# TensorE's order in a step of an attention: value products of blocks 3 to 1 last, transposes of block 0 among the second head's scores

## The chip, the cores and the metric

The kernel runs on one NeuronCore of a Trainium2 chip. The metric is the device time of one execution in microseconds (us), shown as the median of several runs; smaller is better. Five engines work beside each other, each through a queue of its own in order: TensorE (PE in the profile, its weight loads shown apart as PEld), VectorE (DVE), ScalarE (ACT), GpSimd (POOL) and SyncE (SP), which here only issues DMAs.

## The reference

The program is a trunk of two layers over 512 tokens of width 1024 in float32. Layer 0 mixes tokens with a convolution module, layer 1 with an attention in three branches; a gated feed-forward network (FFN) follows each. The change lies in the attention. Cut to what matters:

```
s_s = einsum('bgrqd,bgqkd->bgrqk', qc, k_s) * scale     # selected blocks
p_s = masked_softmax(s_s, tok <= t[:, None])
o_s = einsum('bgrqk,bgqkd->bgrqd', p_s, v_s)
...
s_w = einsum('bgrqd,bgkd->bgrqk', qc, kw) * scale       # window of 512
p_w = masked_softmax(s_w, mask_w)
o_w = einsum('bgrqk,bgkd->bgrqd', p_w, vw)
...
return g[0] * o_c + g[1] * o_s + g[2] * o_w
```

There are 16 query heads of width 64 in 4 groups that share keys and values. At 512 tokens there are 8 blocks to select from and up to 16 may be selected, and the window is as long as the sequence: so the branches "selected" (br = 1) and "window" (br = 2) are both plain causal attentions over all tokens, each with keys and values of its own. The third branch, over 31 compressed blocks (`o_c`), is small.

## The kernel before, in words

The function `nsa` does the attention. After the projections it runs a loop over 16 units, `us`: a unit is one pair of heads `j` (8 pairs) in one branch `br` (1, 2). The two heads of a pair are called first and second here (`par` = 0, 1; `ua`, `ub`). Each head has four rows of 128 queries, t = 0 to 3, and four blocks of 128 keys, kc = 0 to 3; being causal, row t needs keys up to 128(t + 1).

The loop is a software pipeline. Step n makes the scores and the softmax of unit n, the transposes of unit n - 1, the value products of blocks 3, 2 and 1 of unit n - 1 and those of block 0 of unit n - 2. Scores for steps 1 to 15 (unit 0 has its scores ahead of the loop), transposes for steps 1 to 16, and step 17 has only the last value products.

- `score` (L1694) makes one row of scores: two matmuls per row (L1704, L1705; the query operand `St` holds a high and a low part) into a PSUM bank `S`, of which there are three in turn. VectorE adds the mask and finds the row's extreme while it copies the scores to SBUF (L1707, tile `Pm`), ScalarE takes the exponential in place with its sum (L1708). After rows 2 and 0, `weigh` (L1712) takes the reciprocal of two rows' sums on VectorE (L1718), and GpSimd multiplies both rows by it and by the gate (L1722).
- `flip` (L1725) transposes four 128 x 128 pieces of weighed probabilities by TensorE into a PSUM tile `T` (L1735) and copies it to SBUF, tile `t`, by VectorE (L1738) or ScalarE (L1740). `t2` has block 2 of both heads, `t1` blocks 1 and 3 of one head, `t0` block 0 of one head. The PSUM tiles come from a pool of three, `p2`, which the fill work uses too.
- `values` (L1744) multiplies the transposed probabilities with the values into the output `O` (L1761): half as many output partitions per head, the two heads side by side. In units of branch 1 the three products of the compressed branch (L1753 to L1755, operands `pch`, `pcl`) go ahead.
- `run_fill` (L1777) takes the next of five pieces of work for a later pair of heads (`q_pair`, L1473): query moves by DMA on SP's queue (L1485), casts of the operand `St` (L1496, L1498, L1499), scores, softmax and transposes of the compressed branch. A pair's pieces are spread over two and a half steps, two calls a step.

TensorE's order is as written: each of these matmuls is kept in program order (`pe`). What the other engines do, and in which order, is put in order by the compiler's planner from the dependences. So a change of TensorE's order in the text is a change of its queue, and the other queues can change with it.

Behind the loop follow the output projection (`proj_tile`, matmuls `pp`) and the FFN of layer 1.

Of the kernel before, what the change touches and what calls it, by code (L numbers as in the profile page):

```python
# [120 lines left out]
def trunk(ctx: ExitStack, tc: tile.TileContext, A, out):  # L121
    nc = tc.nc
# [8 lines left out]
    def nm(s):  # L131
        cnt[0] += 1
        return f"{s}_{cnt[0]}"
# [78 lines left out]
    def w_hi(i):  # L212
        if i in split or i >= len(units):
            return
        w_dma(i)
        cols = units[i][1]
        hi = wp.tile([P, 1024], F32R, tag="wh", name=f"wh{i}", bufs=2)
        lo = wp.tile([P, 1024], F32R, tag="wl", name=f"wl{i}", bufs=2)
        parted(after(nc.scalar.activation(hi[:, :cols], raws[i][:, :cols], AF.Copy), pin.get(AF)))  # L219
        split[i] = (hi, lo)  # L220

    def w_lo(i=None):
        i = state["next"] if i is None else i
        if i in los or i not in split:
            return
        cols = units[i][1]
        hi, lo = split[i]
        parted(after(nc.vector.tensor_tensor(lo[:, :cols], raws[i][:, :cols], hi[:, :cols], ALU.subtract), pin.get(ALU)))  # L228
        los.add(i)
# [969 lines left out]
    def nsa(acc, gnext):  # L1199
# [481 lines left out]
        def offs(t):  # L1681
            return P * t * (t + 1) // 2
# [11 lines left out]
        def score(U, t):  # L1694
            j, par, br = U["j"], U["par"], U["br"]
            g = 2 * (j // 4) + par
            stk, ks_, kl = qst[j, par], kst[br, g], klo[br, g]
            w = P * (t + 1)
            n = max(w, 256)
            tq = slice(t * P, (t + 1) * P)  # L1700
            mx, sm = U["mx"][:, t:t + 1], U["sm"][:, t:t + 1]
            n_s[0] += 1
            ps = pS[len(pS) > 1 and n_s[0] % 3 == 0].tile([P, T], F32, tag="S", name=nm("S"))
            pe(nc.tensor.matmul(ps[:, :n], stk[:, tq], ks_[:, :n], start=True, stop=False))  # L1704
            pe(nc.tensor.matmul(ps[:, :n], stk[:, tq], kl[:, :n], start=False, stop=True))  # L1705
            Pt = U["P"][:, offs(t):offs(t) + w]
            at_[ALU] = nc.vector.tensor_tensor_reduce(Pt, ps[:, :w], mask[:, T - w:], 1.0, 3e38, ALU.add, ALU.min, mx)  # L1707
            at_[AF] = nc.scalar.activation(Pt, Pt, AF.Exp, bias=mx, scale=-1.0, accum_out=sm)  # L1708
            if t % 2 == 0:
                weigh(U, t)  # L1710
# [14 lines left out]
        def flip(parts, tag, eng):  # L1725

            pt = p2.tile([P, T], F32, tag="p2", name=nm("T"))
            t_ = box["q4"].tile([P, T], F32, tag=tag, name=nm("t"), bufs=2 if tag != "t2" else 1)
            c = 0
            for u, kc in parts:  # L1730
                n = T - P * kc
                u[kc] = t_[:, c:c + n]
                for t in range(kc, 4):
                    o = offs(t) + P * kc
                    pe(nc.tensor.transpose(pt[:, c:c + P], u["P"][:, o:o + P], ident))  # L1735
                    c += P
            if eng is nc.vector:
                eng.tensor_copy(t_, pt)  # L1738
            else:
                eng.activation(t_, pt, AF.Copy)  # L1740
# [3 lines left out]
        def values(Us, kcs):  # L1744


            j, br = Us[0]["j"], Us[0]["br"]
            a = j // 4
            if br == 1 and kcs[0] == 3:
                ob[j] = (p2, pO)[j % 2].tile([P, T], F32, tag="O", name=nm("O"), bufs=1)  # L1750
                ph, pl = pcT[j // 2]
                ch, cl = vcb[a, j % 2]
                pe(nc.tensor.matmul(ob[j], ch, ph, start=True, stop=False))  # L1753
                pe(nc.tensor.matmul(ob[j], ch, pl, start=False, stop=False))
                pe(nc.tensor.matmul(ob[j], cl, ph, start=False, stop=False))  # L1755
            o = ob[j]
            for kc in kcs:
                last = br == 2 and kc == 0
                for par in range(2):
                    g = slice((2 * a + par) * DH, (2 * a + par + 1) * DH)  # L1760
                    pe(nc.tensor.matmul(o[par * 64:par * 64 + 64, P * kc:], vf[br][:, kc, g], Us[par][kc], start=False,  # L1761
                                        stop=last))
                if last:
                    h_ = op.tile([P, T], F32R, tag=f"o{j}", name=nm("oh"))
                    l_ = oha.tile([P, T], F32R, name=nm("ol"))
                    nc.scalar.activation(h_, o, AF.Copy)
                    nc.vector.tensor_tensor(l_, o, h_, ALU.subtract)
                    oh.append(h_)
                    ol.append(l_)
# [7 lines left out]
        def run_fill():  # L1777
            if fill_:
                fill_.pop(0)()

        def start(n):
            nonlocal fill_
            j, br = us[n]
            U[n] = [begin(j, par, br) for par in range(2)]
            if n % 4 == 0 and n // 4 + 1 < 4:
                fill_ = q_pair(n // 4 + 1)
# [13 lines left out]
        for n in range(1, N + 2):  # L1800
            S = n < N
            F = n <= N
            if S:
                start(n)

            def sc_(par, *ts):
                if S:
                    for t in ts:
                        score(U[n][par], t)

            sc_(0, 3, 2)
            if F:
                ua, ub = U[n - 1]
                flip(((ua, 2), (ub, 2)), "t2", nc.scalar)
            if n > 1:
                values(U.pop(n - 2), (0,))
            sc_(0, 1, 0)
            if F:
                flip(((ua, 1), (ua, 3)), "t1", nc.vector)
            sc_(1, 3)  # L1820
            if F:
                flip(((ub, 1), (ub, 3)), "t1", nc.vector)
            sc_(1, 2)
            if n == 1:
                qp0[4]()
            run_fill()
            if F:
                values(U[n - 1], (3, 2, 1))
            sc_(1, 1, 0)
            if F:  # L1830
                flip(((ua, 0),), "t0", nc.scalar)
                flip(((ub, 0),), "t0", nc.scalar)
            run_fill()
            if n in W_AT:
                pin.update(at_)
                if n == W_AT[0]:
                    w_hi(state["next"])
                    w_lo()
# [19 lines left out]
    cx0.close()  # L1858
    acc = ffn(acc, V_NM1, 0)
    acc = nsa(acc, V_NF1)  # L1860
    ffn(acc, None, 1)
    hx[0].close()
# [157 lines left out]
```

## Time and profile before

| | us |
|---|---|
| median of 3 runs | 1239.86 |
| lowest, highest run | 1237.12, 1243.43 |
| the profiled execution, its time | 1243.02 |
| its span in the profile | 1241.2 |
| TensorE busy in the span (8519 matmuls) | 1206.9 (97%) |
| VectorE, ScalarE, GpSimd busy | 903.1, 603.8, 245.3 |
| value products of step 1 / step 15 start at | 703.13 / 835.90 |
| the output projection starts at | 847.72 |

How to read it: a line of the timeline or of the chain is start, duration, engine, line of the kernel, operation, output tile <- input tiles, shape, count; square brackets give the engine's idle time just ahead and the instruction that ended it. A line of the waits is engine, line and what it waited for: us in total, times, longest. A line of groups is line, engine, operation, tiles, shapes, count, busy us, mean ns, idle us ahead and who ended it. Matmuls are pipelined, so their recorded durations overlap; the time that one takes from the next is the difference of two starts.

### The profile page before, as it was taken

What the parts mean: (1) busy time and instruction counts of PE and PEld (TensorE: products, weight loads), DVE (VectorE), ACT (ScalarE), POOL (GpSimd) and SP (SyncE); (2) the same over time, 40 slices, a digit from 0 to 9 for tenths busy, and PEclk for the clock granted to TensorE, in tenths of its full rate; (3) what the DMA queues carried; (4) which work ended last, traced back from release to release, by engine and by line L of the source; (5) the groups of instructions that cost most, each with busy time, mean ns of one, the idle gap of its engine ahead of it and who ended that gap; (6) DMA issues with size and microseconds to landing.
All of it is one profiled execution on the core that took longest, in us unless ns stands there. A gap on an engine that the chain in (4) does not pass through costs nothing.

```text
span 1241.2 us, 22077 instructions
## 1 busy us (share of the span) xinstructions
PE 1206.9 (97%) x8519; PEld 1047.2 (84%) x8519; DVE 903.1 (73%) x1722; ACT 603.8 (49%) x1116; POOL 245.3 (20%) x349
## 2 busy tenths in 40 slices
PE   9999899999999999999998999999999999999998
PEld 6787778799999999887677876667878999998998
DVE  6995598877777576856686787763587777776775
ACT  5221464455555444543443577773354555554443
POOL 2011002011111103102332466552000111110120
PEclk9999999999999999999999899999999999999999
DMA  8748628277777668454266101005323877774882
GB/s 314 264 131 285 172 88 235 92 180 186 181 179 178 162 204 147 97 182 113 60 143 165 26 18 44 1 18 143 112 85 108 198 179 182 190 177 119 225 166 90
DMA packets 88378, 181.11 MB, mean 146 GB/s; under 512 B 36816, under 2 KB 38480, under 8 KB 86736
## 3 DMA queue, kind: packets, MB, share of 16 engines
q1 hardware_dynamic: 66816, 109.99, 29.1%
q0 software_dynamic: 21456, 69.71, 24.8%
q8 instruction: 67, 1.10, 0.4%
q14 instruction: 39, 0.32, 0.1%
HBM read 165.60 MB, written 5.80 MB: 138 GB/s over the span
## 4 chain that ended last, share of the span: by engine, by line
PE 77%; DVE 10%; DMA 3%; issue 3%; ACT 3%; SPq 2%; POOL 1%; DVEq 0%; ACTq 0%; POOLq 0%
PE st L915 27%; PE st L1105 10%; PE pp L281 7%; PE pp L279 7%; PE pp L280 6%; PE O L1761 3%; PE st L281 2%; PE st L280 2%; PE st L279 2%; PE cpe L540 2%; DVE wl L228 1%; DVE Pm L1707 1%; PE T L1735 1%; PE S L1704 1%; DMA rot<-kraw 1%
## 5 line engine op out<-in xcount | busy, mean ns | idle before, releaser
L219 ACT ACTIVATE wh<-wr 128x1024 fp32r<-128x1024 f32 (+4 forms) x150 | 152.8, 1019 | 192.7 <-PE pp L280 64.2
L228 DVE TENSOR_TENSOR wl<-wr,wh 128x1024 fp32r<-128x1024 f32 (+4 forms) x150 | 179.9, 1199 | 44.0 <-ACT wh L219 43.5
L915 PE MATMUL st<-bh,sl 128*128 128x256 f32 x680 | 192.6, 283 | 1.1 <-DVE sl L899 1.1
L915 PE MATMUL st<-bh,sh 128*128 128x256 f32 x680 | 192.7, 283 | 0.0
L915 PE MATMUL st<-bl,sh 128*128 128x256 f32 x680 | 192.0, 282 | 0.0
L281 PE MATMUL pp<-hh,wl 128*128 128x512 f32 x400 | 157.6, 397 | 4.4 <-DVE wl L228 4.4
L279 PE MATMUL pp<-hh,wh 128*128 128x512 f32 x400 | 158.9, 400 | 2.6 <-ACT wh L219 2.3
L280 PE MATMUL pp<-hl,wh 128*128 128x512 f32 x400 | 158.0, 396 | 0.0
L915 PEld LDWEIGHTS st<-bh,sl 128*128 128x128 f32 x680 | 130.2, 192 | 1.5 <-DVE sl L899 1.5
L915 PEld LDWEIGHTS st<-bl,sh 128*128 128x128 f32 x680 | 130.6, 192 | 0.1
L915 PEld LDWEIGHTS st<-bh,sh 128*128 128x128 f32 x680 | 130.0, 191 | 0.1
L899 DVE TENSOR_TENSOR sl<-S,sh 128x512 fp32r<-128x512 f32 x136 | 88.0, 689 | 51.7 <-ACT sh L898 51.7
L281 PEld LDWEIGHTS pp<-hh,wl 128*128 128x128 f32 x400 | 75.2, 188 | 23.9 <-DVE wl L228 6.9
L279 PEld LDWEIGHTS pp<-hh,wh 128*128 128x128 f32 x400 | 75.3, 188 | 23.6 <-ACT wh L219 4.8
L1722 POOL TENSOR_SCALAR Pm<-Pm,sm,gates 128x512 f32<-128x512 f32 (+3 forms) x128 | 80.8, 645 | 64.6 <-DVE sm L1718 54.2
L280 PEld LDWEIGHTS pp<-hl,wh 128*128 128x128 f32 x400 | 75.4, 188 | 18.1 <-issue 1.1
L1708 ACT ACTIVATE Pm<-Pm,mx 128x512 f32<-128x512 f32 (+3 forms) x128 | 71.1, 557 | 38.3 <-DVE mx L1707 35.8
L1707 DVE CUSTOM_DVE_ANT_0 Pm<-S,mask 128x512 f32<-128x512 f32 (+3 forms) x128 | 59.3, 484 | 28.8 <-PE S L1705 28.1
L1105 PE MATMUL st<-oz,soh 128*128 128x256 f32 x448 | 79.5, 280 | 0.0
L898 ACT ACTIVATE sh<-S 128x512 fp32r<-128x512 f32 x136 | 77.6, 620 | 0.0
L915 PE MATMUL st<-bl,wh 128*128 128x256 f32 x272 | 76.2, 280 | 0.0
L915 PE MATMUL st<-bh,wl 128*128 128x256 f32 x272 | 76.1, 280 | 0.0
(308 smaller groups left out, 2813.9 us busy)
## 6 DMA issues: line engine op xcount, KB each, us to landing
S<-fw_x POOLq DMA_DIRECT2D x68, 512.0 KB, 5.9
wr<-fw_in SPq DMA_DIRECT2D x46, 512.0 KB
So<-fw_q POOLq DMA_DIRECT2D x38, 448.0 KB, 6.4
bd<-bands POOLq DMA_DIRECT2D x12, 1280.0 KB, 12.6
wr<-fw_q SPq DMA_DIRECT2D x24, 448.0 KB
r<-fw_x SPq DMA_DIRECT2D x34, 256.0 KB
wr<-fw_p SPq DMA_DIRECT2D x16, 512.0 KB
wr<-cw_in SPq DMA_DIRECT2D x14, 512.0 KB
```

The costliest lines, as they stand in the source:

```text
L219: parted(after(nc.scalar.activation(hi[:, :cols], raws[i][:, :cols], AF.Copy), pin.get(AF)))
L228: parted(after(nc.vector.tensor_tensor(lo[:, :cols], raws[i][:, :cols], hi[:, :cols], ALU.subtract), pin.get(ALU)))
L279: held(nc.tensor.matmul(ps, wh, xh, start=first, stop=False))
L280: held(nc.tensor.matmul(ps, wh, xl, start=False, stop=False))
L281: held(nc.tensor.matmul(ps, wl, xh, start=False, stop=last))
L898: pe(nc.scalar.activation(h_[:, c], z, AF.Copy))
L899: pe(nc.vector.tensor_tensor(l_[:, c], z, h_[:, c], ALU.subtract))
L915: pe(nc.tensor.matmul(ps[:, :H], p_[:, k], m_[c][:, t], start=first and c == 0 and q == 0, stop=last and c == 3 and q == 2, skip_group_che ...
L1105: pe(nc.tensor.matmul(ps, a[:, c], b[:, t], start=p in (1, 4) and i == 0 and r == 0, stop=i == NO - 1 and r == 2, skip_group_check=True))
L1707: at_[ALU] = nc.vector.tensor_tensor_reduce(Pt, ps[:, :w], mask[:, T - w:], 1.0, 3e38, ALU.add, ALU.min, mx)
L1708: at_[AF] = nc.scalar.activation(Pt, Pt, AF.Exp, bias=mx, scale=-1.0, accum_out=sm)
L1722: nc.gpsimd.tensor_scalar(Pt, Pt, sm[:, k:k + 1], gates[:, t + k, br * 16 + h:br * 16 + h + 1], ALU.mult, ALU.mult)
```

## The change

In a step, TensorE's order was: ... scores of the second head's row 2, first fill call, value products of blocks 3, 2, 1, scores of the second head's rows 1 and 0, transposes of block 0 of the first and of the second head, second fill call. Now it is: ... scores of the second head's row 2, transposes of block 0 of the first head, scores of the second head's rows 1 and 0, transposes of block 0 of the second head, first fill call, value products of blocks 3, 2, 1, second fill call. The instructions are the same ones.

```diff
             sc_(1, 2)
             if n == 1:
                 qp0[4]()
+            if F:
+                flip(((ua, 0),), "t0", nc.scalar)
+            sc_(1, 1, 0)
+            if F:
+                flip(((ub, 0),), "t0", nc.scalar)
             run_fill()
             if F:
                 values(U[n - 1], (3, 2, 1))
-            sc_(1, 1, 0)
-            if F:
-                flip(((ua, 0),), "t0", nc.scalar)
-                flip(((ub, 0),), "t0", nc.scalar)
             run_fill()
             if n in W_AT:
                 pin.update(at_)
```

## The prediction

> **What bounds it.** I read the page's chain first, then the busy table of the attention steps, then the waits there, then the timeline of one step.
>
> ```profile
> span 1241.2 us, 22077 instructions
> PE 77%; DVE 10%; DMA 3%; issue 3%; ACT 3%; SPq 2%; POOL 1%; DVEq 0%; ACTq 0%; POOLq 0%
> core 0: us, PE busy (x) PEld busy (x) DVE busy (x) ACT busy (x) POOL busy (x), PEclk, DMA share, GB/s
> 804.00:816.00 12.00, 11.47 (x66) 7.27 (x65) 7.67 (x31) 9.68 (x27) 6.75 (x10) 1.00 0.06 10
> 950.00:1050.00 100.00, 99.47 (x829) 99.05 (x828) 77.00 (x131) 52.97 (x98) 17.76 (x20) 1.00 0.74 183
> ```
>
> TensorE carries the chain. In the attention steps it runs at the full granted clock (1.00) and looks 96% busy, but that counts pipelined ends; waits have to be read from starts. After the attention it is 99% busy, so what the attention saves should reach the end whole.
>
> ```profile
> 703.13 1.45 PE O L1761 x12
> 835.90 1.51 PE O L1761 x9
> PEld O L1761 <- DVE t L1738: 7.7, 11, 1.1
> PEld O L1761 <- ACT t L1740: 3.4, 7, 1.0
> PEld O L1754 <- DVE pcl L1546: 0.7, 1, 0.7
> ```
>
> The first two rows (the chain) are the value products of step 1 and step 15: 14 steps in 132.8 us, 9.48 us each. The others (waits between 696 and 840 us: total, times, longest) are TensorE's weight loads standing still: 7.7 us ahead of the products of blocks 3 to 1, for VectorE's copies of the transposes; 3.4 us ahead of block 0's products, for ScalarE's copies. Step 12 shows how they arise:
>
> ```profile
> 806.47 0.60 PE L1735 MATMUL T<-cc,Pm 128*128 128x128 f32 x4
> 806.82 0.42 PE L1704 MATMUL S<-kst,St 128*128 128x384 f32 x1
> 807.48 0.68 DVE L1738 COPY t<-T 128x512 f32<-128x512 f32 x1
> 808.22 0.84 PEld L1761 LDWEIGHTS O<-t,v 128*64 128x64 f32 x10 [0.68 <-DVE t L1738]
> 808.74 0.61 ACT L1708 ACTIVATE Pm<-Pm,mx 128x384 f32<-128x384 f32 x1 [0.32 <-DVE mx L1707]
> 809.66 0.38 PE L1704 MATMUL S<-kst,St 128*128 128x256 f32 x1
> 809.81 1.42 POOL L1722 TENSOR_SCALAR Pm<-Pm,sm,gates 128x512 f32<-128x512 f32 x2 [0.28 <-DVE sm L1718]
> 810.24 1.03 PE L1735 MATMUL T<-cc,Pm 128*128 128x128 f32 x8
> 811.03 0.48 PE L1704 MATMUL S<-kst,St 128*128 128x512 f32 x1
> 811.93 0.60 PE L1735 MATMUL T<-cc,Pm 128*128 128x128 f32 x4
> 813.62 0.19 PEld L1761 LDWEIGHTS O<-t,v 128*64 128x64 f32 x2 [0.97 <-ACT t L1740]
> ```
>
> The second head's transposes issue at 806.47, VectorE gets to their copy at 807.48, and the ten remaining value products start at 808.22 after 0.68 us of standing. Only then come the second head's scores of rows 1 and 0 (809.66) and the eight transposes of block 0 (810.24), up to 811.03. That block is 811.03 - 809.66 = 1.37 us of TensorE work that needs no value product.
>
> **The change, part by part.** No instruction is added or removed; the 1.37 us block goes ahead of the value products of blocks 3 to 1 (1.44 us, 808.22 to 809.66).
>
> Wait for VectorE's copies: each now has 1.37 us of other work ahead of it, and the longest wait is 1.1. All 7.7 us go, and in step 1 the 0.7 us for `pcl` too.
>
> Wait for ScalarE's copies of block 0: the copies are made as before, but 1.44 us of products now lie between their transposes and their use; the longest wait is 1.0. All 3.4 us go. A second effect goes with it:
>
> ```profile
> 717.40 1.22 PE O L1761 x4
> 726.68 1.50 PE O L1761 x4
> 766.38 1.01 PE O L1761 x4
> 784.81 1.51 PE O L1761 x4
> 803.84 1.22 PE O L1761 x4
> ```
>
> The same four products of block 0 take 1.01 us when both heads' copies are there and up to 1.51 when the second comes late, since the heads then no longer overlap. The four slower ones lose 0.2 + 0.5 + 0.5 + 0.2 = 1.4 us; that goes.
>
> The end of the attention, where no scores are left:
>
> ```profile
> 843.39 1.51 PE L1761 MATMUL O<-t,v 128*64 128x128 f32 x10 [0.17 <-DVE t L1738]
> 844.83 1.09 PE L1735 MATMUL T<-cc,Pm 128*128 128x128 f32 x8
> 846.23 1.56 PE L1761 MATMUL O<-t,v 128*64 128x512 f32 x4 [0.31 <-ACT t L1740]
> ```
>
> The eight transposes move into the wait before 843.39, and block 0's products follow at 844.83 instead of 846.23: 1.4 us.
>
> Gain so far 7.7 + 0.7 + 3.4 + 1.4 + 1.4 = 14.6 us.
>
> What comes next: the block-2 transposes of the following step need the second head's rows 3 and 2 weighed by GpSimd. That chain starts at the scores of row 2 and is not moved, while TensorE reaches the transposes sooner.
>
> ```profile
> 759.71 0.42 PE L1704 MATMUL S<-kst,St 128*128 128x384 f32 x1
> 765.94 0.44 PE L1735 MATMUL T<-cc,Pm 128*128 128x128 f32 x2 [0.75 <-POOL Pm L1722]
> 769.15 0.42 PE L1704 MATMUL S<-kst,St 128*128 128x384 f32 x1
> 816.45 0.42 PE L1704 MATMUL S<-kst,St 128*128 128x384 f32 x1
> 820.52 1.43 POOL Pm L1722 x2
> 822.00 0.44 PE T L1735 x2
> ```
>
> In step 12 the chain takes from 806.82 to 811.23 (809.81 + 1.42), 4.4 us; TensorE's own work over the same stretch is the row-2 scores 0.4, the block 1.37, the products 1.5, two scores 0.9 (811.03 to 811.93) and the first head's two transposes 0.2, together 4.4: even. In step 13, whose products have three more ahead (0.8) and whose VectorE has one more copy, the chain takes 816.45 to 822.00, 5.55, against 5.2: 0.35 short. In step 7, with fill work, it takes 6.23, and TensorE waits there already. I take 0.25 us a step on average, 14 x 0.25 = 3.5 us of new wait. Bounds: none (the full 14.6 stays) and, above, a delay that eats everything (first rival).
>
> ScalarE's copy of the first head's block 0 is now ready about when the exponentials of rows 3 and 2 are. It can go ahead of row 2's: 0.58 us less the 0.32 us that ScalarE stands idle there (808.74), some 0.2 in half the steps, 1.4 us.
>
> The first fill call moves behind the same 1.37 us, with its compressed-branch scores, query moves on SP's queue and operand casts:
>
> ```profile
> 706.66 43.63 SPq L1485 DMA_DIRECT2D q<-qraw  x12
> ACT St L1498 <- PE S L1705: 6.9, 5, 3.3
> ```
>
> The twelve moves are issued up to 750.29 in bursts well ahead of use; the casts do not wait for them but for the old operand's last scores, 6.9 us in five casts. Those scores come earlier now, so the delay costs nothing; were the cover gone, 1.37 us in each of the six steps that start casts, 8 us, would stand on ScalarE. PSUM banks: the last scores need those of rows 0 and 3 drained and the second transposes the first copy's bank; both drains stand ahead, in VectorE's program order, of the copy that the products wait for today, so the moved block can't wait longer than they do now.
>
> Sum: 14.6 - 3.5 - 1.4 = 9.7, say 10 us. The profiled execution took 1243.02 us (span 1241.2), so it would take 1233; it lies 3.2 us above the median 1239.86, against which the forecast is 1230.
>
> **The rivals.** First, the wait only changes its name (no change). Period by the GpSimd chain: from the second head's transposes of block 2 to the next row-2 scores is 769.15 - 765.94 = 3.21 us; with the chain's 4.5 (light step) or 5.55 that gives 7.7 and 8.8, mean 8.2, against 9.48 now. A delay of 1.25 us a step on the chain would give all back: 1240. For it: step 7's chain is 6.23 us long, and 6.23 + 3.21 is the present period. Against it: only that one step is so long in the rows shown.
>
> Second, slower: row 2's exponential and reciprocal get behind what is brought forward, in the queues of the two engines that feed GpSimd: two copies of 0.585 on ScalarE (first row below) and on VectorE two score reductions with their read-outs (0.42 in the second row, and half of it for the narrower one, with two short read-outs 0.8). That is 2.0 us a step: period 10.2, 0.7 us x 14 = 10 us longer, 1250. It decides from 1.25 us a step on.
>
> ```profile
> L1740 ACT ACTIVATE t<-T 128x512 f32<-128x512 f32 x47 | 26.9, 585 | 7.5 <-PE T L1735 7.5
> L1707 DVE CUSTOM_DVE_ANT_0 Pm<-S,mask 128x256 f32<-128x256 f32 x30 | 12.7, 423 | 19.4 <-PE S L1705 19.2
> L1499 DVE TENSOR_TENSOR St<-q,St x10: 684/690/2571, 706.0 to 787.3; 64x512 fp32r<-64x512 f32 x10
> ```
>
> Against it: VectorE stood waiting for scores 19.2 us ahead of just these reductions, so there is room, and the reciprocal is due only after row 2's exponential (0.6), by when two reductions are nearly through.
>
> Third, VectorE's operand subtractions (last row: least, median, longest ns) fall on GpSimd's weighing more often. One took 2.57 us instead of 0.69. If all ten did, VectorE would lose 10 x 1.89 less the 2.9 lost already (9.8 us busy in all, 6.9 at the median), 16 us; on the path in full, 10 - 16 = 6 us longer, 1246. The Trainium skill, "SBUF — State Buffer", section "Who interferes with whom", states the mechanism: a VectorE instruction with two SBUF inputs and a GpSimd instruction that reads SBUF exclude each other through a shared port. By that rule such a collision is a matter of who issues first, which the change reshuffles. For now the median of 0.69 speaks for rare hits.
>
> Fourth, nothing comes next: 14.6 us and more, 1224.
>
> **How the numbers follow.** My forecast (6 to 13 us gained, 1227 to 1234) has 0.57, the full gain 0.13, the changed name 0.16, the collisions 0.04, slower 0.10. The range 1221 to 1242 takes in the full gain with the spread of three runs and no change, and leaves out the slower cases and part of the edges. A measurement of this kernel can tell about 0.5% (6 us) from no change: faster by more, 0.69 (0.13 and nearly all of 0.57); slower by more, 0.10; within, 0.21.
>
> **What would show it.** Right: no wait of the value products for VectorE's copies above 0.2 us; block 0's products at 1.0 us throughout; the step near 8.8 us; attention's end some 10 us earlier with the same stretch behind it. The next wait should stand at the block-2 transposes, for GpSimd. Wrong: that wait at 1 us or more in most steps; ScalarE's copies ahead of row 2's exponential; subtractions of 2 us and over; or a gain in the attention that the later projection gives back.

## The result, and the profile after

| | before | after |
|---|---|---|
| median of the runs beside each other (5 and 5), us | 1238.84 | 1230.37 |
| lowest to highest, us | 1237.12 to 1243.43 | 1229.74 to 1231.71 |
| span of the profiled execution, us | 1241.2 | 1229.9 |

The ratio after to before is 0.9945, 95% interval 0.9922 to 0.9967; in a second series on another occasion 0.9933 (0.9914 to 0.9952). The forecast was 1230.

First the timeline of TensorE: the first scores of step 1 and the first matmul of the output projection, of the kernel before and then of the kernel after (start, duration).

```profile
695.80 0.39 PE L1704 MATMUL S<-kst,St 128*128 128x512 f32 x1
847.72 0.50 PE L279 MATMUL pp<-oh,wh 128*128 128x512 f32 x1
```

```profile
694.34 0.39 PE L1704 MATMUL S<-kst,St 128*128 128x512 f32 x1
836.67 0.50 PE L279 MATMUL pp<-oh,wh 128*128 128x512 f32 x1
```

The attention took 847.72 - 695.80 = 151.9 us and takes 836.67 - 694.34 = 142.3: 9.6 us less. Behind it lie 393.5 us of the span before and 393.2 after, so nothing is given back there. Most of the rest of the difference between the spans, 1.5 us, stands ahead of step 1, where nothing was changed.

The waits of the kernel after, between 696 and 840 us, and under them the rows of the kernel before for the same wait at the transposes:

```profile
PEld T L1735 <- POOL Pm L1722: 8.6, 10, 1.6
PE T L1735 <- POOL Pm L1722: 6.2, 8, 1.3
PEld O L1761 <- issue: 6.6, 30, 0.4
PEld O L1761 <- ACT Pm L1708: 0.2, 1, 0.2
```

```profile
PEld T L1735 <- POOL Pm L1722: 1.5, 3, 1.0
PE T L1735 <- POOL Pm L1722: 0.8, 1, 0.8
```

No wait of the value products for the copies `t` is left, neither VectorE's (7.7 us before) nor ScalarE's (3.4 us). By the starts in the timelines, from the first product of a group to the work behind the group, the value products of the attention took 55.2 us and take 39.1: each group of twelve took 1.45 to 2.8 us and takes 1.45. What grew is the wait of the block-2 transposes for GpSimd's weighed rows, from 0.8 to 6.2 us on TensorE itself, from 1.5 to 8.6 by the weight loads. The weight loads of the moved scores also stand longer for VectorE to drain their PSUM banks (`PEld S L1704 <- DVE mx L1707`, 1.4 us before and 7.4 after), but TensorE itself waits 0.4 us there in both kernels. The chain of the kernel after shows the main two things:

```profile
702.35 1.45 PE O L1761 x12
721.79 1.92 POOL Pm L1722 x2
723.76 0.44 PE T L1735 x2
724.20 1.01 PE O L1761 x4
797.59 1.01 PE O L1761 x4
803.96 1.43 POOL Pm L1722 x2
805.44 0.44 PE T L1735 x2
```

Each block-0 product of the chain takes 1.01 us, where it took up to 1.5 on the chain (and up to 2.2 by the starts, in steps 7 and 13). Ahead of the transposes stands GpSimd (721.79, 803.96), which was hardly on the chain there before. And the end of the attention, in TensorE's timeline, now runs without a gap from the last transposes through all sixteen value products into the projection:

```profile
832.28 2.16 PE L1735 MATMUL T<-cc,Pm 128*128 128x128 f32 x16
834.37 2.37 PE L1761 MATMUL O<-t,v 128*64 128x128 f32 x16
836.67 0.50 PE L279 MATMUL pp<-oh,wh 128*128 128x512 f32 x1
```

### The profile page after: what moved, and what is told of

Read it like the earlier page. It is cut to its first block, busy times and chain, and to the rows that moved or that the text cites. A ratio compares the mean times of both kernels' runs of the same rounds, so it can differ in the third digit from the quotient of the medians.

```text
span 1229.9 us, 22075 instructions
## 1 busy us (share of the span) xinstructions
PE 1198.9 (97%) x8519; PEld 1043.2 (85%) x8519; DVE 901.0 (73%) x1722; ACT 602.3 (49%) x1116; POOL 246.5 (20%) x349
## 4 chain that ended last, share of the span: by engine, by line
PE 78%; DVE 7%; ACT 3%; DMA 3%; issue 3%; POOL 3%; SPq 2%; DVEq 0%; ACTq 0%; POOLq 0%
PE st L915 27%; PE st L1105 10%; PE pp L281 7%; PE pp L279 7%; PE pp L280 6%; PE st L281 2%; PE st L280 2%; PE st L279 2%; PE cpe L540 2%; PE O L1761 2%; PE T L1735 2%; POOL Pm L1722 1%; DVE wl L228 1%; PE S L1704 1%; PE S L1705 1%
## 5 line engine op out<-in xcount | busy, mean ns | idle before, releaser
L915 PE MATMUL st<-bh,wh 128*128 128x256 f32 x272 | 76.1, 280 | 0.0
```

What stands on the lines that cost most here:

```text
L915: pe(nc.tensor.matmul(ps[:, :H], p_[:, k], m_[c][:, t], start=first and c == 0 and q == 0, stop=last and c == 3 and q == 2, skip_group_che ...
```

## The experiments

Since the stretch behind the attention has the same length in every profile (393.2 to 393.6 us), the attention is compared by its own length in the profile, from the first scores of step 1 to the projection, beside the timed ratios, which also contain what varies ahead of the attention. The rows of waits in this section are those between 694 and 838 us. "Chain" below is the time in a step from the second head's row-2 scores to the end of GpSimd's weighing of rows 3 and 2.

| kernel | attention, us | against before | timed ratio (95%) |
|---|---|---|---|
| before | 151.9 | | |
| after; once more | 142.3; 142.3 | -9.6; -9.6 | 0.9945; 0.9933 (0.9914 to 0.9952) |
| scores only | 145.2 | -6.7 | 0.9939 (0.9921 to 0.9957) |
| transposes only | 143.7 | -8.3 | 0.9942 (0.9927 to 0.9956) |
| after, block 2 later | 137.2 | -14.7 | 0.9872 (0.9853 to 0.9892) |
| after, copies behind | 140.5 | -11.4 | 0.9911 (0.9888 to 0.9934) |
| after, rows unweighed | 134.6 | -17.3 | 0.9882 (0.9862 to 0.9901) |
| after, both | 138.0 | -13.9 | 0.9890 (0.9873 to 0.9907) |
| before, block 2 later | 154.6 | +2.7 | 1.0025 (1.0013 to 1.0036) |

**The two halves of the change.** Scores only:

```diff
             sc_(1, 2)
 ...
+            sc_(1, 1, 0)
             run_fill()
             if F:
                 values(U[n - 1], (3, 2, 1))
-            sc_(1, 1, 0)
             if F:
                 flip(((ua, 0),), "t0", nc.scalar)
                 flip(((ub, 0),), "t0", nc.scalar)
```

> Of the change only the second head's scores of rows 1 and 0 go ahead of the value products; the transposes of block 0 stay behind them. Theory (cover): the waits of the value products go as far as other TensorE work lies ahead of them. The scores are 0.58 us of the 1.37 us moved, the eleven waits for VectorE's copies are 0.7 us on average, so some 6 of 7.7 us go and 1 to 2 us stay; ScalarE's 3.4 us ahead of block 0's products and the slow end (1.4 us) stay: 5 us faster than before, 1234, with a wait for VectorE's copies of 1 to 2 us and for ScalarE's of 3 us or more. Rival (operands): the gain comes from the early scores, because ScalarE's casts of the query operands no longer stand for them (6.9 us before): then this part brings the whole gain, 1230, and casts wait under 2 us.

Measured: median 1229.25 beside 1236.6 before. Its waits:

```profile
PEld T L1735 <- POOL Pm L1722: 4.0, 5, 1.1
PEld O L1761 <- ACT t L1740: 1.9, 8, 0.5
PEld O L1761 <- DVE t L1738: 1.0, 2, 0.6
```

VectorE's copies are waited for 1.0 us instead of 7.7, as the theory of cover has it; ScalarE's 1.9 us, less than expected. The attention gains 6.7 us, more than the expected 5 and two thirds of the whole. The casts don't wait at all here, so this run alone doesn't rule out the rival. The other half does, transposes only:

```diff
             sc_(1, 2)
 ...
+            if F:
+                flip(((ua, 0),), "t0", nc.scalar)
+                flip(((ub, 0),), "t0", nc.scalar)
             run_fill()
             if F:
                 values(U[n - 1], (3, 2, 1))
             sc_(1, 1, 0)
-            if F:
-                flip(((ua, 0),), "t0", nc.scalar)
-                flip(((ub, 0),), "t0", nc.scalar)
```

> Of the change only the transposes of block 0 of both heads go ahead of the value products; the second head's scores of rows 1 and 0 stay behind them. Theory (cover): 0.8 us lies ahead of the value products now, so the waits for VectorE's copies all but go (under 1 us left), the waits for ScalarE's copies of block 0 go (1.44 us of products between), the end of the attention gets its 1.4 us: 9 us faster than before, 1230, like the whole change. Rival (operands): the scores come no earlier than before, the casts stand as before, little gain: 1236 to 1239.

Measured: median 1229.4 beside 1236.6.

```profile
ACT St L1498 <- PE S L1705: 6.8, 5, 3.0
PEld T L1735 <- POOL Pm L1722: 4.5, 9, 1.1
PEld O L1761 <- DVE t L1738: 0.4, 1, 0.4
```

The casts of the query operands stand for the scores 6.8 us, as before the change (6.9), and the attention is 8.3 us shorter all the same. So the gain of this half does not come from the casts; both halves gain as the waits for copies fall, whichever instructions give the cover. How much of the first half's gain the casts have is not shown. The halves bring 6.7 and 8.3 us and together 9.6, not 15: either of them takes most of the waits for copies away, and in both the wait for GpSimd at the transposes has grown (4.0 and 4.5 us, from 1.5), which takes back a part.

**What is late now.** Block 0's products, for which nothing is awaited any more, ahead of block 2's transposes:

```diff
             sc_(0, 3, 2)
+            if n > 1:
+                values(U.pop(n - 2), (0,))
             if F:
                 ua, ub = U[n - 1]
                 flip(((ua, 2), (ub, 2)), "t2", nc.scalar)
-            if n > 1:
-                values(U.pop(n - 2), (0,))
```

> The changed kernel, and the products of block 0 of the unit before go ahead of the transposes of block 2, so that GpSimd's weighed rows 3 and 2 are needed 1.0 us later. Theory (GpSimd's chain is what is late now; TensorE waits 6.2 us for it at these transposes): most of it goes, 4 to 5 us faster than the changed kernel, 1225, wait at the transposes under 2 us. Rival (ScalarE and VectorE are at their own limit in a step, the wait only moves on): 1230 as the changed kernel, with the 5 us standing in front of other work.

Measured: median 1221.37 beside 1236.6, and 5.1 us less attention than the kernel after.

```profile
PEld T L1735 <- POOL Pm L1722: 11.0, 15, 0.8
PE T L1735 <- POOL Pm L1722: 0.4, 1, 0.4
PEld O L1761 <- ACT Pm L1708: 1.0, 4, 0.3
```

The two rows for the same wait must be read together: the weight loads of the transposes still stand 11.0 us, but while the products of block 0 are still running; TensorE itself waits 0.4 us instead of 6.2. GpSimd's rows were what was late. Of all variants that compute the whole, this one has the shortest attention and the lowest median, 15 us under the kernel before (ratio 0.9872); its interval overlaps with that of both edits together (below).

The same place without GpSimd's work there. Rows 3 and 2 of the second head are left unscaled:

```diff
             for k in (1, 0):
+                if par == 1 and t == 2:
+                    continue
                 w = P * (t + k + 1)
```

> The changed kernel without GpSimd's weighing of rows 3 and 2 of the second head (left out: these rows are used unscaled); nothing else changes place. Theory (GpSimd's chain is what TensorE waits for at the transposes of block 2): the chain loses GpSimd's 1.43 us, the 6.2 us of waiting there all but go, 5 us faster than the changed kernel. Rival (the chain is late already at ScalarE's exponential, or the wait moves on to other work): 2 us or less, with a wait for ScalarE in its place.

Measured: median 1220.7 beside 1236.95; 7.7 us less attention than after, between the 6.2 us that TensorE and the 8.6 us that its weight loads waited there. In the groups of its trace (idle ahead and its ender last; the line numbers are two higher):

```profile
L1737 PE MATMUL T<-cc,Pm 128*128 128x128 f32 x309 | 46.2, 272 | 0.0
L1737 PEld LDWEIGHTS T<-cc,Pm 128*128 128x128 f32 x308 | 36.9, 140 | 4.5 <-POOL Pm L1724 1.4 <-issue 0.2
```

TensorE's wait at the transposes is gone (0.0; 1.4 us of weight loads are left) and none for ScalarE took its place, against the rival. With two of its eight weighings a step left out GpSimd is also freer for the rest, which this run doesn't separate.

**Why the chain got longer.** In the kernel after, the planner put one or both of ScalarE's copies of block 0 ahead of the second head's row-2 exponential. Step 14 of the kernel after:

```profile
817.28 0.42 PE L1704 MATMUL S<-kst,St 128*128 128x384 f32 x1
818.61 0.54 DVE L1707 CUSTOM_DVE_ANT_0 Pm<-S,mask 128x384 f32<-128x384 f32 x1
818.77 1.14 ACT L1740 ACTIVATE t<-T 128x512 f32<-128x512 f32 x2
819.81 0.60 ACT L1708 ACTIVATE Pm<-Pm,mx 128x384 f32<-128x384 f32 x1
820.87 2.47 POOL L1722 TENSOR_SCALAR Pm<-Pm,sm,gates 128x512 f32<-128x512 f32 x4 [0.89 <-DVE sm L1718]
822.35 0.44 PE L1735 MATMUL T<-cc,Pm 128*128 128x128 f32 x2 [0.44 <-POOL Pm L1722]
```

Row 2's reduction ends at 819.15, but two copies hold ScalarE from 818.77, and its exponential starts at 819.81; then GpSimd, then the transposes, which waited. Before, in step 12, this exponential started 0.04 us after the reduction (808.16 + 0.54, 808.74). In this experiment both copies are ordered behind it (`row2` is that exponential; `after` only orders):

```diff
             if F:
-                flip(((ua, 0),), "t0", nc.scalar)
+                row2 = at_[AF]
+                flip(((ua, 0),), "t0", nc.scalar, row2)
             sc_(1, 1, 0)
             if F:
-                flip(((ub, 0),), "t0", nc.scalar)
+                flip(((ub, 0),), "t0", nc.scalar, row2)
```

> The changed kernel, and ScalarE's two copies of block 0 are ordered behind the second head's row-2 exponential; in the changed kernel's queue one or both stand ahead of it in most steps. Theory (the chain to GpSimd's weighing got longer by these copies, from 4.4 to 5.0 us in the light steps, 0.6 us): the chain is 4.4 us again, the wait at the transposes of block 2 falls by 0.4 us in half of the steps, 3 us faster than the changed kernel: 1227. Rival (the copies only fill ScalarE's waiting time; GpSimd is the late one by itself): 1230, wait unchanged. If the copies then come too late for block 0's products, a wait for ScalarE shows ahead of those.

Measured: median 1226.1 beside 1236.6 (runs from 1221.19 to 1229.66); 1.8 us less attention than after. Step 14 of it, and its waits:

```profile
807.93 0.42 PE L1704 MATMUL S<-kst,St 128*128 128x384 f32 x1
809.19 0.55 DVE L1707 CUSTOM_DVE_ANT_0 Pm<-S,mask 128x384 f32<-128x384 f32 x1
809.78 0.62 ACT L1708 ACTIVATE Pm<-Pm,mx 128x384 f32<-128x384 f32 x1 [0.32 <-DVE mx L1707]
810.40 1.06 ACT L1740 ACTIVATE t<-T 128x512 f32<-128x512 f32 x2
810.86 1.42 POOL L1722 TENSOR_SCALAR Pm<-Pm,sm,gates 128x512 f32<-128x512 f32 x2 [1.08 <-DVE sm L1718]
```

```profile
PEld T L1735 <- POOL Pm L1722: 7.4, 8, 1.5
PE T L1735 <- POOL Pm L1722: 5.0, 7, 1.3
```

The chain of step 14 is 5.0 us long in the kernel after (weighing of both rows done at 822.29) and 4.35 here (812.28). Over steps 2 to 15 its mean was 5.07 us before, is 5.53 after, and 5.15 here. So the copies do lengthen it by some 0.4 us a step; but the attention gains 1.8 us and not 3, and 5.0 of the 6.2 us of waiting stay. The theory is right in kind and the larger part of the new wait is not the copies. The chain is longest in the steps with fill work (6.9 us in steps 5 and 9, here as after).

The traces place most of the rest there. Of the 6.2 us that TensorE waits at these transposes in the kernel after, 3.6 are three waits, those for the chains of steps 5, 7 and 9 (they end at 743.28, 761.06 and 780.57); with the copies behind, the same three have 3.7 of the 5.0 us. Step 5 on the chain of the kernel after, and then GpSimd's timeline in step 5 of the kernel before:

```profile
739.31 0.56 POOL St L1496
739.86 1.68 POOL Pm L1722 x3
742.13 1.10 POOL Pm L1722
743.28 0.44 PE T L1735 x2
```

```profile
740.88 3.81 POOL L1722 TENSOR_SCALAR Pm<-Pm,sm,gates 128x512 f32<-128x512 f32 x6
744.61 0.63 POOL L1496 CAST St<-q 128x512 fp32r<-128x512 f32 x1
```

`St` is fill work: the cast of a query operand (0.6 us), one that GpSimd makes. Like ScalarE's casts it needs the old operand's last scores, which now come earlier, and in steps 5 and 9 it has got ahead of the weighing of the second head's rows 3 and 2, where before it came behind them. (In step 7 it stood ahead before the change too, and TensorE waited there already.) It does not come alone: VectorE's subtractions follow such a cast, and beside them two of the weighings take 1.08 and 1.09 us here, where the same shapes have a median of 0.56 and 0.67. In every profile with the scores moved early and all rows weighed, the scores-only run among them, the cast stands ahead in steps 5 and 9 and the chain there is 6.9 us long; in the three with the scores late (before, transposes only, block 2 later alone) it stands behind and the chain is 5.4. In the scores-only run 2.5 of TensorE's 2.8 us of waiting at the transposes belong to steps 5, 7 and 9; in transposes only it waits for none of these three chains. That the planner puts it there because of the early scores is read from this pattern; what moving this one cast back would bring was not run.

Both edits together, on the kernel after:

> The changed kernel with block 0's products ahead of block 2's transposes, and ScalarE's two copies of block 0 behind the row-2 exponential. Theory: with block 2 later, TensorE waits only 0.4 us for GpSimd, so a chain 0.6 us shorter has little left to bring: 1221 as with block 2 later alone, within 2 us. Rival (both delays are on the path one after the other): 3 us faster again, 1218. A wait of block 0's products for the later copies would make it slower than 1221.

Measured: median 1222.87 beside 1236.95, attention 138.0 us against 137.2 with block 2 later alone.

```profile
PE T L1735 <- POOL Pm L1722: 0.7, 2, 0.4
PEld O L1761 <- ACT Pm L1708: 1.8, 7, 0.3
```

No further gain: once the transposes come late enough, a shorter chain buys nothing, as the theory expected. By the starts, block 0's products take 1.01 us here as they do with block 2 later alone, so no wait for the later copies shows; what the other 0.8 us of attention are, one profile of each doesn't tell.

**The order of the two edits.** Block 2 later, on the kernel before:

> The kernel before, with only block 0's products ahead of block 2's transposes. Theory (before the change TensorE waits for the copies, not for GpSimd; 1.5 us in all at the transposes of block 2): the products of block 0 now follow their transposes 0.5 us sooner, so their wait for ScalarE's copies grows from 3.4 us by up to 0.5 us in each of seven steps and more, the wait for VectorE's copies stays at 7 us or more: no gain, 1237 to 1241. Rival (block 2 late is a gain by itself): 5 us faster than before, 1232.

Measured: median 1240.04 beside 1236.95, slower by 0.25% (0.13% to 0.36%), attention 2.7 us longer.

```profile
PEld O L1761 <- ACT t L1740: 13.1, 27, 1.4
PEld O L1761 <- DVE t L1738: 7.0, 13, 1.1
```

The edit that brings 5.1 us behind the change loses 2.7 ahead of it: there block 0's products stand for ScalarE's copies, and taking the transposes from ahead of them takes their cover (the wait grows from 3.4 to 13.1 us of weight loads standing, over the whole attention from 4.9 to 14.0; more than was expected).

The kernel after once more, beside these:

> The changed kernel once more, beside the variants of this series, so that they are compared on one chip. All theories: 7 to 9 us faster than before, as in its first measurement (ratio 0.9945); in the profile the attention from step 1's first scores to the output projection takes 142 us against 152.

Measured: median 1228.55 beside 1236.95, attention 142.3 us again, 8.5 us of weight loads waiting for GpSimd. The steps repeat.

## Why the prediction was right, step by step

- **VectorE's and ScalarE's copies** (7.7 and 3.4 us): both waits went whole. The half changes show that cover does it: 0.58 us of scores or 0.8 us of transposes each take most of them.
- **Products of the two heads side by side** (1.4 us): all at 1.01 us, as expected.
- **The end** (1.4 us): behind the starts below (before, then after) both kernels have the same 16 transposes and 16 products up to the projection. They take 847.72 - 841.35 = 6.37 us before and 836.67 - 832.28 = 4.39 after, 2.0 us less.

```profile
841.35 1.09 PE L1735 MATMUL T<-cc,Pm 128*128 128x128 f32 x8
```

```profile
832.28 2.16 PE L1735 MATMUL T<-cc,Pm 128*128 128x128 f32 x16
```

- **`pcl`** (0.7 us): that wait is gone from the products, in step 1.
- **New wait at the block-2 transposes** (3.5 us) and **ScalarE's copy ahead of row 2** (1.4 us), 4.9 together: the place was right, the size too small. By the weight loads, in which the gains were counted too, the wait grew from 1.5 to 8.6 us, by 7.1. The copies' part, taken away, is worth 1.8 us. Its size in a step was taken too small: the copies delay row 2's exponential in nearly every step, not in half of them, and two of them can stand ahead of it (from the end of the reduction to the exponential it is 0.06 us in the mean of steps 2 to 15 before, 0.71 after). The fill work, put at nothing because the old operand's scores come earlier, was not free either: with the scores early, GpSimd's cast stands ahead of the weighing in two steps, as said above.
- **The sum.** Forecast were 14.6 us gross (13.9 without `pcl`) and 4.9 given back; the products alone gained 55.2 - 39.1 = 16.1, and 7.1 were given back at the transposes. Both sides were some 2 us too small, so that 9.7 forecast and 9.6 measured lie this close is partly luck; the mechanism, and which wait comes next, were right.
- **The period** was forecast at 8.8 us; it is (828.34 - 702.35) / 14 = 9.00. The 9.48 before was read a little too long: of the twelve products of step 15 the first two start at 835.12 and the other ten, after a wait, at 835.90, so it was (835.12 - 703.13) / 14 = 9.43. The steps gave less and the end gave more than was said. Before, and then after:

```profile
835.12 0.43 PE L1761 MATMUL O<-t,v 128*64 128x128 f32 x2
```

```profile
828.34 1.52 PE L1761 MATMUL O<-t,v 128*64 128x128 f32 x12
```

- **The rivals.** The slower one named the right queue: the copies did get ahead of the exponential on ScalarE. VectorE's reductions did not lengthen the chain with them, and it grew by 0.46 us a step (5.07 to 5.53), where 1.25 would have been needed to lose the gain. The third rival is half true: VectorE lost no more by it, its ten subtractions took 9.8 us before and 8.2 after, but GpSimd did, the 128 weighings took 80.8 us before and 83.0 after, and some of the longer ones lie on the chain, as in step 5.

```profile
L1499 DVE TENSOR_TENSOR St<-q,St 64x512 fp32r<-64x512 f32 x10 | 8.2, 816 | 0.3
```

The Trainium skill, "SBUF — State Buffer", section "Who interferes with whom", holds that such a subtraction and a GpSimd instruction that reads SBUF exclude each other. The trace fits that where the two meet: the weighing of 1.09 us starts at 742.13, while a subtraction of 1.16 us runs (from 741.52). None of the variants tested the rule itself.

## What to carry to other kernels

In an in-order queue a wait can be removed, without removing work, by putting ready work ahead of it; count for each wait how much ready work there is and what it is worth, and expect two such edits not to add up, because the next chain takes over. So ask what becomes late next before the first edit is made: the second edit here was worth 5 us behind the first and cost 2.7 without it. And when one engine's order is changed by hand, look at what the planner does with the other queues: work that comes free early can get ahead of work on the critical chain, here ScalarE's copies and GpSimd's cast.

## What the runs showed that was not expected

Much of what separates two runs of these kernels stands ahead of the attention. In ten profiles step 1's first scores start between 685.8 and 695.8 us, though nothing ahead of them was changed, while the stretch behind the attention takes 393.2 to 393.6 us in all, and the attention of the changed kernel 142.3 us twice. So lengths of stages seem to tell differences of 1 us apart, which the medians, with runs several us from each other, do not; only the changed kernel was profiled twice, though.

A part of what varies can be read in the profiles. Between 660 and 692 us, just ahead of these scores, the granted clock of TensorE was 0.79 in the two profiles whose scores start latest (before and after, 695.8 and 694.3 us) and 0.95 in the three that start earliest (685.8 to 688.1), with the others between; on average it was 1.00 ahead of that stretch and 1.00 in the attention. In 32 us, 0.16 of the clock is 5 of the 10 us. Why it differs there, and where the other 5 us lie, was not looked into.
